# Adding pending squares on VectorE ahead of the norm sums, and the last store on ScalarE's queue

## The chip, the core and the metric

One NeuronCore of a Trainium2 chip runs the kernel: TensorE (PE, matmuls and their weight loads), VectorE (DVE), ScalarE (ACT), GpSimd (POOL) and the queues that issue DMAs, among them SyncE's (SP). The engines run side by side, each through its own instructions in order, and wait for each other by semaphores. The metric is the device time of one execution in microseconds; the median of several runs is given.

## What is computed

A two-layer decoder trunk on 512 tokens of width 1024, in float32. Layer 0 mixes by sliding-window attention and a convolution, layer 1 by a state-space scan; behind each mixer stands a gated ConvFFN, and at the end an RMS norm. What matters here are the norms, one behind each mixer and each ConvFFN:

```python
def rmsnorm(x, g):
    xf = x.astype(jnp.float32)
    y = xf * lax.rsqrt(jnp.mean(xf * xf, axis=-1, keepdims=True) + NORM_EPS)
    return (y * g.astype(jnp.float32)).astype(x.dtype)
...
        h = rmsnorm(x, norm_mix[i]) * (1.0 + sc_m) + sh_m
        ...
        x = x + g_m * y
        h = rmsnorm(x, norm_ffn[i]) * (1.0 + sc_f) + sh_f
        x = x + g_f * conv_ffn(h, ffn_w_gate[i], ffn_conv_w[i], ffn_conv_b[i],
                               ffn_w_val[i], ffn_w_down[i])
    return rmsnorm(x, final_norm)
```

## The kernel before

The residual stream `x` lies transposed in on-chip memory: 8 tiles of 128 features by 512 tokens. A weight tile comes by DMA as float32 (`raw`); ScalarE rounds it to a coarser type (`wh`, L317) and VectorE makes the rest (`wl`, L322). A product of one weight tile and one activation tile is three matmuls (L370 to L372: high times high, high times low, low times high).

Between two phases stands `boundary` (L476), called four times: behind the mixer of layer 0, its ConvFFN, the mixer of layer 1, and the last ConvFFN, where the final norm and the stores follow. It gets the weights of the phase's last output tiles (four behind a mixer, two behind a ConvFFN), and works them off twice, for the first 256 tokens (half 0) and the second 256 (half 1), so that the norm of half 0 can run beside the products of half 1.

- `products` (L486) makes one output tile of one half on TensorE. `finish` (L495) adds it to `x` on VectorE (L474, `residual`), and has ScalarE square the new `x` (L501) into a fresh tile. The squares are added up in `acc` (tile `ssq`), which already holds those of the phase's earlier output tiles. `finish` adds the square of the tile before (L499, VectorE), except behind the last tile: so two squares per half are still pending when the norm begins, those of the last two output tiles, in the list `sq[hf]`.
- `norm_steps` (L505) is a generator of the norm's small steps. Its first step calls `token_sums` (L391) on `acc` and the pending squares: for each source tile and each of the two groups of 128 tokens of the half, a matmul with a column of ones (L396), six matmuls into one PSUM tile of 128 by 2. Each such matmul shows as two passes in the trace. Then ScalarE takes the root (L508), VectorE refines its inverse by a Newton step (L510 to L516), and TensorE spreads the result over all partitions (L404).
- The first four steps for half 0 are issued out of `products` of half 1, once a quarter of its matmuls are issued (`SUMS_AT` 0.25), the spread at 0.65 (`REST_AT`). Just before, `W.ahead()` (L522) prepares the next weight tiles, which puts L317 on ScalarE's queue and L322 on VectorE's.
- The norm of half 1 is begun behind the last residual and two groups of the next phase's first matmuls (`first`, which makes three output tiles). Between its steps the modulated tiles `hn` of half 0 are made (`fill`, L460 on VectorE, L461 on ScalarE, L467 on VectorE).
- In the last boundary `fill` is that of `final` (L1818): per half, GpSimd multiplies two of the eight output tiles, VectorE the other six (L1828), in pairs. SP's queue stores the pairs of VectorE (L1832), in half 1 the last pair as two single tiles (L1830); ScalarE's queue stores GpSimd's pair (L1834).

PE, ACT, DVE and POOL run what the program issues in the order in which it is written (`manual_schedule`).

Of the kernel before, what the change touches and what calls it, by code (L numbers as in the profile page):

```python
# [21 lines left out]
ALU = mybir.AluOpType  # L22
# [202 lines left out]
def trunk(ctx: ExitStack, tc: tile.TileContext, xT_d, vecs_d, rows_d, dsk_d, pos_d, const_d, wss_d, wg0_d,  # L225
          w_d, wmod_d, wdt_d, out_d):
    nc = tc.nc
# [11 lines left out]
    def nm(s):  # L239
        uid[0] += 1  # L240
        return f"{s}{uid[0]}"

    def tmp(shape=(P, T), dt=F32):
        return tp.tile(list(shape), dt, tag="tmp", name=nm("tmp"))

    def bank(shape=(P, T)):
        return pp.tile(list(shape), F32, tag="ps", name=nm("ps"))

    def small(n, dt=F32):
        return sp.tile([P, n], dt, tag="sm", name=nm("sm"), bufs=24)  # L250
# [9 lines left out]
    tt = nc.vector.tensor_tensor  # L260
# [108 lines left out]
    def mm3(ps, w, ah, al, first, last):  # L369
        mm(ps, lhsT=w[0], rhs=ah, start=first, stop=False)  # L370
        mm(ps, lhsT=w[0], rhs=al, start=False, stop=False)  # L371
        mm(ps, lhsT=w[1], rhs=ah, start=False, stop=last)  # L372
# [9 lines left out]
    def step(gen, n=1):  # L382
        for _ in range(n):
            next(gen, None)

    def drain(gen):
        for _ in gen:
            pass


    def token_sums(srcs, n=NCH):  # L391

        ps = bank((P, n))
        for k, t_ in enumerate(srcs):
            for c in range(n):
                mm(ps[:, c:c + 1], lhsT=t_[:, c * P:(c + 1) * P], rhs=ones,  # L396
                   start=(k == 0 and c == 0), stop=(k == len(srcs) - 1 and c == n - 1))
        return ps

    def spread(col, n=NCH):  # L400

        ps = bank((P, n * P))
        for c in range(n):
            mm(ps[:, c * P:(c + 1) * P], lhsT=col[:, c:c + 1].broadcast_to([P, P]), rhs=ident,  # L404
               start=True, stop=True)
        return ps
# [31 lines left out]
    HALF = (slice(0, T // 2), slice(T // 2, T))  # L438
# [34 lines left out]
    def residual(ps, m, gate, hs=slice(0, T)):  # L473
        stt(x[:, m, hs], ps, gate(m), x[:, m, hs], ALU.mult, ALU.add)  # L474

    def boundary(ws, ms, acts, gate, acc, nxt, after=None):  # L476

        n = len(acts)
        ms = list(ms)
        sq = [[], []]
        ss, y = [None, None], [None, None]

        def products(hf, i, at=None):  # L486
            hs = HALF[hf]
            o = bank((P, T // 2))
            for kt in range(n):
                mm3(o, ws[i][kt], acts[kt][0][:, hs], acts[kt][1][:, hs], kt == 0, kt == n - 1)  # L490
                if at is not None:
                    at((i * n + kt + 1) / (len(ws) * n))
            return o

        def finish(hf, i, o):  # L495
            hs = HALF[hf]
            residual(o, ms[i], gate, hs)
            if len(sq[hf]) > 1 or (sq[hf] and i < len(ws) - 1):
                tt(acc[:, hs], acc[:, hs], sq[hf].pop(0), ALU.add)  # L499
            sq[hf].append(tmp((P, T // 2)))  # L500
            act(sq[hf][-1], x[:, ms[i], hs], AF.Square)  # L501
            if after is not None:
                after(ms[i], hs)

        def norm_steps(hf):  # L505
            s_ = token_sums([acc[:, HALF[hf]], *sq[hf]], 2)
            sd, v, y_, a, y2 = (small(2) for _ in range(5))
            act(sd, s_, AF.Sqrt, scale=1.0 / 1024.0, bias=eps[:, 0:1])  # L508
            yield
            ts(v, s_, 1.0 / 1024.0, 1e-6, ALU.mult, ALU.add)  # L510
            nc.vector.reciprocal(y_, sd)
            tt(a, y_, y_, ALU.mult)
            yield
            stt(a, a, -0.5, v, ALU.mult, ALU.mult)
            yield
            stt(y2, a, 1.5, y_, ALU.add, ALU.mult)  # L516
            yield
            y[hf] = spread(y2, 2)

        for i in range(len(ws)):  # L520
            finish(0, i, products(0, i))
        W.ahead()  # L522
        norm0 = norm_steps(0)
        hn, fill, nfirst = nxt()

        def at(f):
            if f >= SUMS_AT and ss[0] is None:
                ss[0] = True
                step(norm0, 4)
            if f >= REST_AT and y[0] is None:  # L530
                step(norm0)

        for i in range(len(ws)):
            o = products(1, i, at)
            if i < len(ws) - 1:
                finish(1, i, o)
        fill0 = fill(0, y[0])
        step(fill0, 3)
        finish(1, len(ws) - 1, o)
        wf = [W.take_only() for _ in range(nfirst)]  # L540
        outs = [bank() for _ in range(nfirst)]

        def first(hf, kt):
            hs = HALF[hf]
            for o_, w in zip(outs, wf):
                mm3(o_[:, hs], w[kt], hn[kt][0][:, hs], hn[kt][1][:, hs], kt == 0, kt == KT - 1)

        norm1 = norm_steps(1)
        if nfirst:
            first(0, 0)  # L550
            first(0, 1)
        step(norm1)
        step(fill0)
        if not nfirst:
            drain(fill0)
        for _ in range(3):
            step(norm1)
            step(fill0)
        drain(fill0)
        if nfirst:  # L560
            for kt in range(2, 5):
                first(0, kt)
        step(norm1)
        if nfirst:
            for kt in range(5, KT):
                first(0, kt)
        fill1 = fill(1, y[1])
        for kt in range(KT):
            step(fill1)
            if nfirst:  # L570
                first(1, kt)
        drain(fill1)
        return hn, outs
# [1244 lines left out]
    def final(fp):  # L1818
        def fill(hf, rb):
            hs = HALF[hf]  # L1820
            rs = fp.tile([P, T // 2], F32, tag="rs", name=nm("rs"), bufs=2)
            nc.scalar.copy(rs, rb)
            os_ = [fp.tile([P, 2, T // 2], F32, tag="o", name=nm("o"), bufs=8) for _ in range(4)]
            for k in range(2):
                nc.gpsimd.tensor_tensor(os_[0][:, k, :], x[:, k, hs], rs, ALU.mult)
            for n, kt in enumerate(range(2, 8)):
                o = os_[kt // 2]
                tt(o[:, kt % 2, :], x[:, kt, hs], rb, ALU.mult)  # L1828
                if hf and n > 3:
                    nc.sync.dma_start(out_d[:, kt:kt + 1, hs], o[:, kt % 2:kt % 2 + 1, :])  # L1830
                elif kt % 2:
                    nc.sync.dma_start(out_d[:, kt - 1:kt + 1, hs], o)  # L1832
                yield
            nc.scalar.dma_start(out_d[:, 0:2, hs], os_[0])  # L1834
        return None, fill, 0

    ctx.enter_context(tc.manual_schedule(engines={getattr(mybir.EngineType, e) for e in MANUAL}))
# [126 lines left out]
```

## Time and profile before

| | |
|---|---|
| median of 3 runs | 1341.47 us (1340.62 to 1342.1) |
| the profiled execution | 1342.0 us, span 1340.2 us |
| TensorE busy | 1313.2 us, 98% |
| VectorE busy | 875.1 us, 65% |
| ScalarE busy | 597.0 us, 45% |
| GpSimd busy | 74.7 us, 6% |
| mean granted clock of TensorE | 0.99 |

Times in the profile count from the first instruction of the profiled execution; its own time is 1.8 us longer than that span. A busy engine counts the time in which an instruction of it runs, and matmuls overlap: one of 256 columns shows 0.28 us and the next starts 0.12 us later. The four boundaries' norms lie at about 212, 578, 958 and 1324 us.

### The profile page before, as it was taken

How to read it: one execution, taken by the hardware profiler on the slowest of the kernel's cores; microseconds unless marked ns; L12 is line 12 of the kernel's file. 1: busy time of each engine (PE TensorE's matmuls, PEld its weight loads, DVE VectorE, ACT ScalarE, POOL GpSimd, SP SyncE). 2: the span in 40 equal slices, each digit the busy share in tenths (PEclk: the TensorE clock that was granted, in tenths of full speed). 3: DMA queues.
4: the chain of work that ended last, by engine and by line, in shares of the span. 5: the costliest groups of instructions: out<-in, count | busy, mean ns of one | idle time of the engine just before them, and what ended most of it. 6: DMA issues, size and time to landing. Idle time of an engine off the chain costs nothing.

```text
span 1340.2 us, 17613 instructions
## 1 busy us (share of the span) xinstructions
PE 1313.2 (98%) x6873; PEld 1078.0 (80%) x6873; DVE 875.1 (65%) x1342; ACT 597.0 (45%) x947; POOL 74.7 (6%) x129
## 2 busy tenths in 40 slices
PE   7999899999999999999999999999999999999997
PEld 6856589888888888897888887887988888888886
DVE  6976987775666676568686775878665434434443
ACT  4624734432233233347694764836353313322333
POOL 7010000000000000100110100000000000000002
PEclk8999899999999999999999999999999999999999
DMA  9773363564664665223542432342223233233311
GB/s 341 236 266 103 128 210 111 170 222 152 215 194 149 218 203 180 89 68 95 166 139 84 139 110 97 122 123 79 64 94 115 89 111 94 83 92 112 99 56 63
DMA packets 56436, 183.64 MB, mean 137 GB/s; under 512 B 7008, under 2 KB 10144, under 8 KB 56352
## 3 DMA queue, kind: packets, MB, share of 16 engines
q1 hardware_dynamic: 51536, 170.24, 39.5%
q0 software_dynamic: 4128, 11.61, 2.6%
q8 instruction: 54, 0.88, 0.3%
q10 hardware_dynamic: 688, 0.66, 0.1%
q14 instruction: 30, 0.25, 0.1%
HBM read 179.21 MB, written 3.28 MB: 136 GB/s over the span
## 4 chain that ended last, share of the span: by engine, by line
PE 93%; DVE 3%; ACT 2%; DMA 1%; issue 1%; DVEq 0%; ACTq 0%; POOLq 0%
PE ps L370 27%; PE ps L371 27%; PE ps L372 27%; PE ps L798 2%; PE ps L950 2%; PE ps L1643 1%; DMA M<-scr 1%; PE ps L1621 1%; PE ps L404 1%; PE ps L396 1%; PE ps L1609 1%; ACT M L1593 0%; PE ps L419 0%; PE ps L1108 0%; PE ps L1635 0%
## 5 line engine op out<-in xcount | busy, mean ns | idle before, releaser
L370 PE MATMUL ps<-hn,wh 128*128 128x512 f32 (+1 forms) x1214 | 460.2, 379 | 0.8 <-ACT hn L461 0.8
L371 PE MATMUL ps<-hn,wh 128*128 128x512 f32 (+1 forms) x1214 | 454.1, 374 | 0.4
L372 PE MATMUL ps<-hn,wl 128*128 128x512 f32 (+1 forms) x1214 | 453.9, 374 | 0.0
L322 DVE TENSOR_TENSOR wl<-raw,wh 128x1024 fp32r<-128x1024 f32 (+1 forms) x208 | 250.9, 1209 | 95.1 <-ACT wh L317 93.8
L317 ACT CAST wh<-raw 128x1024 fp32r<-128x1024 f32 (+1 forms) x208 | 213.1, 1027 | 221.5 <-PE ps L371 216.1
L370 PEld LDWEIGHTS ps<-hn,wh 128*128 128x128 f32 x1214 | 228.5, 188 | 44.6 <-issue 3.5
L371 PEld LDWEIGHTS ps<-hn,wh 128*128 128x128 f32 x1214 | 228.7, 188 | 42.3 <-issue 1.9
L372 PEld LDWEIGHTS ps<-hn,wl 128*128 128x128 f32 x1214 | 228.5, 188 | 40.7
L474 DVE SCALAR_TENSOR_TENSOR x<-ps,modv,x 128x512 f32<-128x512 f32 (+1 forms) x108 | 73.9, 690 | 115.2 <-PE ps L372 115.2
L370 PE MATMUL ps<-fh,wh 128*128 128x512 f32 (+1 forms) x380 | 142.2, 374 | 0.0
L371 PE MATMUL ps<-fl,wh 128*128 128x512 f32 (+1 forms) x380 | 141.9, 373 | 0.0
L372 PE MATMUL ps<-fh,wl 128*128 128x512 f32 (+1 forms) x380 | 141.9, 373 | 0.0
L595 DVE SCALAR_TENSOR_TENSOR mr<-mr,cb 128x1024 f32<-128x1024 f32 x92 | 111.1, 1219 | 1.6 <-DMA mr<-in_wmod_dram 1.6
L1346 ACT ACTIVATE tmp<-ps,vecs 128x512 f32<-128x512 f32 x44 | 34.2, 777 | 114.8 <-PE ps L372 114.8
L1347 DVE SCALAR_TENSOR_TENSOR tmp<-ps,vecs,tmp 128x511 f32<-128x511 f32 x44 | 32.9, 749 | 79.6 <-ACT tmp L1346 79.6
L370 PEld LDWEIGHTS ps<-fh,wh 128*128 128x128 f32 x380 | 71.5, 188 | 12.8
L372 PEld LDWEIGHTS ps<-fh,wl 128*128 128x128 f32 x380 | 71.5, 188 | 12.7
L371 PEld LDWEIGHTS ps<-fl,wh 128*128 128x128 f32 x380 | 71.5, 188 | 12.6
L295 ACT CAST fh<-tmp 128x512 fp32r<-128x512 f32 x44 | 27.3, 620 | 96.4 <-DVE tmp L1351 95.6
L449 POOL TENSOR_TENSOR ssq<-ssq,tmp 128x512 f32<-128x512 f32 x10 | 13.4, 1337 | 909.8 <-ACT tmp L448 909.8
L1349 ACT ACTIVATE tmp<-tmp 128x512 f32<-128x512 f32 x44 | 27.8, 632 | 75.6 <-DVE tmp L1348 75.5
L1593 ACT ACTIVATE M<-M,acs 128x128 f32<-128x128 f32 x128 | 39.6, 389 | 24.4 <-DMA M<-scr 24.3
(291 smaller groups left out, 1462.1 us busy)
## 6 DMA issues: line engine op xcount, KB each, us to landing
raw<-in_w_dram SPq DMA_DIRECT2D x176, 512.0 KB, 3.7
mr<-in_wmod_dram SPq DMA_DIRECT2D x80, 512.0 KB, 3.7
raw<-in_w_dram SPq DMA_DIRECT2D x32, 448.0 KB, 3.4
mr<-in_wss_dram SPq DMA_DIRECT2D x16, 512.0 KB, 7.2
M<-scr POOLq DMA_DIRECT2D x16, 512.0 KB, 4.6
s<-uc SPq DMA_DIRECT2D x16, 266.0 KB, 5.2
raw<-in_wg_dram SPq DMA_DIRECT2D x8, 384.0 KB, 7.5
E<-scr POOLq DMA_DIRECT2D x32, 96.0 KB, 3.7
```

The costliest lines, as they stand in the source:

```text
L295: nc.scalar.copy(h, src)
L317: nc.scalar.copy(h, self.raw[i].rearrange("p (k m) -> p k m", m=P))
L322: eng.tensor_tensor(l, self.raw[i].rearrange("p (k m) -> p k m", m=P), h.bitcast(F32), ALU.subtract)
L370: mm(ps, lhsT=w[0], rhs=ah, start=first, stop=False)
L371: mm(ps, lhsT=w[0], rhs=al, start=False, stop=False)
L372: mm(ps, lhsT=w[1], rhs=ah, start=False, stop=last)
L474: stt(x[:, m, hs], ps, gate(m), x[:, m, hs], ALU.mult, ALU.add)
L595: stt(raw, raw, 1.0, mod_pool[2], ALU.mult, ALU.mult, accum_out=out)
L1346: act(c, pg, AF.Identity, bias=vec("fcb", i), scale=vec("fcw", 3 * i + 2))
L1347: stt(c[:, 1:], pg[:, :T - 1], vec("fcw", 3 * i + 1), c[:, 1:], ALU.mult, ALU.add)
L1349: act(c, c, AF.Silu)
L1593: act(m_[:, i, c, :], m_[:, i, c, :], AF.Relu, bias=acs[:, c, h:h + 1], scale=-1.0)
```

## The change

At the start of `norm_steps`, VectorE adds pending squares into `acc` until none is left in half 0, and one in half 1. `token_sums` then has one source in half 0 (two matmuls in place of six) and two in half 1 (four in place of six). In half 1 of the last boundary, GpSimd's pair is stored ahead of the last single tile, and that tile's store goes to ScalarE's queue too.

```diff
         def norm_steps(hf):
+            while len(sq[hf]) > hf:
+                tt(acc[:, HALF[hf]], acc[:, HALF[hf]], sq[hf].pop(0), ALU.add)
             s_ = token_sums([acc[:, HALF[hf]], *sq[hf]], 2)
...
                 tt(o[:, kt % 2, :], x[:, kt, hs], rb, ALU.mult)
+                if hf and n == 5:
+                    nc.scalar.dma_start(out_d[:, 0:2, hs], os_[0])
                 if hf and n > 3:
-                    nc.sync.dma_start(out_d[:, kt:kt + 1, hs], o[:, kt % 2:kt % 2 + 1, :])
+                    (nc.scalar if n == 5 else nc.sync).dma_start(out_d[:, kt:kt + 1, hs], o[:, kt % 2:kt % 2 + 1, :])
                 elif kt % 2:
                     nc.sync.dma_start(out_d[:, kt - 1:kt + 1, hs], o)
                 yield
-            nc.scalar.dma_start(out_d[:, 0:2, hs], os_[0])
+            if not hf:
+                nc.scalar.dma_start(out_d[:, 0:2, hs], os_[0])
```

Lines behind L505 move down by two, so the new adds are L507, the root L510 and the Newton step L512 to L518.

VectorE in the first boundary, from the residual of half 0's last tile (L474) on. `wl_2066` is the rest of a weight tile, `ssq_129` is `acc`, `tmp_2039` and `tmp_2055` are the two pending squares. Before:

```order
L474 SCALAR_TENSOR_TENSOR x<-ps_2041,modv,x 128x256
L322 TENSOR_TENSOR wl_2066<-raw_2057,wh_2065 128x1024
L510 TENSOR_SCALAR sm_2106<-ps_2098 128x2
L511 RECIPROCAL sm_2107<-sm_2105 128x2
L512 TENSOR_TENSOR sm_2108<-sm_2107 128x2
```

and after the change:

```order
L474 SCALAR_TENSOR_TENSOR x<-ps_2041,modv,x 128x256
L322 TENSOR_TENSOR wl_2066<-raw_2057,wh_2065 128x1024
L507 TENSOR_TENSOR ssq_129<-ssq_129,tmp_2039 128x256
L507 TENSOR_TENSOR ssq_129<-ssq_129,tmp_2055 128x256
L512 TENSOR_SCALAR sm_2104<-ps_2100 128x2
L513 RECIPROCAL sm_2105<-sm_2103 128x2
```

The two adds stand behind the weight split L322 and ahead of the Newton step. TensorE at the same place, where `ps_2085` is half 1's first tile, `ps_2098` the sums and `ps_2119` half 1's second tile. Before:

```order
L371 MATMUL ps_2085<-s_1611,wh_1835 128x256
L372 MATMUL ps_2085<-s_1610,wl_1836 128x256
L396 MATMUL ps_2098<-ones,ssq_129 128x1 x2
L396 MATMUL ps_2098<-ones,tmp_2039 128x1 x2
L396 MATMUL ps_2098<-ones,tmp_2055 128x1 x2
L370 MATMUL ps_2119<-s_1560,wh_1835 128x256
```

and after (the sums are `ps_2100`, the second tile `ps_2117`):

```order
L371 MATMUL ps_2085<-s_1611,wh_1835 128x256
L372 MATMUL ps_2085<-s_1610,wl_1836 128x256
L396 MATMUL ps_2100<-ones,ssq_129 128x1 x2
L370 MATMUL ps_2117<-s_1560,wh_1835 128x256
L371 MATMUL ps_2117<-s_1561,wh_1835 128x256
```

Four matmuls of the sums are gone; the two that are left read `ssq_129`, which the second add writes. The end of ScalarE's queue, with the spread's copy (L1822 before) and the store of GpSimd's pair of half 1. Before:

```order
L1834 DMA out_dram<-o_10763 128x2x256
L1822 COPY rs_10804<-ps_10801 128x256
L1834 DMA out_dram<-o_10806 128x2x256
L1959 UNCONDITIONAL_BRANCH
```

and after:

```order
L1839 DMA out_dram<-o_10752 128x2x256
L1824 COPY rs_10792<-ps_10789 128x256
L1832 DMA out_dram<-o_10794 128x2x256
L1834 DMA out_dram<-o_10797 128x256
L1964 UNCONDITIONAL_BRANCH
```

The store of the last single tile (`o_10797`) stands behind that of GpSimd's pair (`o_10794`).

## Rows read from the trace of the kernel before

**Rows 1.** The page's busy table: busy us (share of span), instructions.
```profile
PE 1313.2 (98%) x6873; PEld 1078.0 (80%) x6873; DVE 875.1 (65%) x1342; ACT 597.0 (45%) x947; POOL 74.7 (6%) x129
```

**Rows 2.** Timeline, first boundary: start us, us, engine, line, operation [idle before it <-releaser].
```profile
211.36 0.42 ACT L501 ACTIVATE tmp<-x 128x256 f32<-128x256 f32 x1 [1.08 <-DVE x L474]
211.69 1.03 ACT L317 CAST wh<-raw 128x1024 fp32r<-128x1024 f32 x1
212.00 0.50 PE L396 MATMUL ps<-ones,ssq 128*128 128x1 f32 x4
212.36 1.03 PE L396 MATMUL ps<-ones,tmp 128*128 128x1 f32 x8
212.75 1.23 DVE L322 TENSOR_TENSOR wl<-raw,wh 128x1024 fp32r<-128x1024 f32 x1 [1.48 <-ACT wh L317]
...
213.26 0.37 PE L370 MATMUL ps<-s,wh 128*128 128x256 f32 x1
```

**Rows 3.** Timeline, second and third boundary, half 0: sums and weight split.
```profile
577.88 0.50 PE L396 MATMUL ps<-ones,ssq 128*128 128x1 f32 x4
...
578.61 1.23 DVE L322 TENSOR_TENSOR wl<-raw,wh 128x1024 fp32r<-128x1024 f32 x1 [1.48 <-ACT wh L317]
...
957.76 0.50 PE L396 MATMUL ps<-ones,ssq 128*128 128x1 f32 x4
...
958.49 1.23 DVE L322 TENSOR_TENSOR wl<-raw,wh 128x1024 fp32r<-128x1024 f32 x1 [1.48 <-ACT wh L317]
```

**Rows 4.** Instructions on tile `ssq`: count, ns min/median/max, first and last start us.
```profile
L499 DVE TENSOR_TENSOR ssq<-ssq,tmp x8: 415/418/426, 208.3 to 963.0; 128x256 f32<-128x256 f32 x8
```

**Rows 5.** Timeline, first boundary, half 0: root, last Newton step, spread.
```profile
214.03 0.26 ACT L508 ACTIVATE sm<-ps,eps 128x2 f32<-128x2 f32 x1
...
214.98 0.16 DVE L516 SCALAR_TENSOR_TENSOR sm<-sm,sm 128x2 f32<-128x2 f32 x1
...
215.83 0.61 PE L404 MATMUL ps<-con,sm 128*128 128x128 f32 x4
```

**Rows 6.** Timeline, first boundary, half 1: last residual, sums, Newton's first step.
```profile
220.60 0.48 DVE L474 SCALAR_TENSOR_TENSOR x<-ps,modv,x 128x256 f32<-128x256 f32 x1
...
221.29 0.50 PE L396 MATMUL ps<-ones,ssq 128*128 128x1 f32 x4
...
223.02 0.16 DVE L510 TENSOR_SCALAR sm<-ps 128x2 f32<-128x2 f32 x1 [1.16 <-ACT sm L508]
```

**Rows 7.** Timeline, last boundary: half 0's square and table load, half 1's residual and sums.
```profile
1323.00 0.42 ACT L501 ACTIVATE tmp<-x 128x256 f32<-128x256 f32 x1 [1.62 <-DVE x L474]
...
1323.98 1.28 ACT L508 ACT_TABLE_LOAD   x1
...
1329.23 0.48 DVE L474 SCALAR_TENSOR_TENSOR x<-ps,modv,x 128x256 f32<-128x256 f32 x1
...
1330.27 0.61 PE L396 MATMUL ps<-ones,tmp 128*128 128x1 f32 x4 [0.30 <-ACT tmp L501]
```

**Rows 8.** Timeline: SP's last stores; then windows: us, busy by engine, PEclk, DMA share, GB/s.
```profile
1335.15 1.52 SPq L1830 DMA_DIRECT2D out_dram<-o  x2
...
1335.00:1338.00 3.00, 0.00 (x0) 0.00 (x0) 0.32 (x1) 0.00 (x0) 0.00 (x0) 0.50 1.03 339
1338.00:1340.00 2.00, 0.00 (x0) 0.00 (x0) 0.00 (x0) 0.00 (x0) 0.00 (x0) 0.50 0.02 5
```

**Rows 9.** Windows: us, busy (x) of PE, PEld, DVE, ACT, POOL, PEclk, DMA share, GB/s.
```profile
152.00:156.00 4.00, 0.61 (x8) 0.23 (x6) 3.93 (x10) 2.92 (x5) 0.00 (x0) 1.00 0.83 286
156.00:168.00 12.00, 11.20 (x56) 7.53 (x58) 11.42 (x29) 10.02 (x27) 0.00 (x0) 0.57 0.40 121
218.00:220.00 2.00, 1.44 (x10) 1.03 (x10) 1.82 (x6) 1.37 (x3) 0.00 (x0) 1.00 0.28 63
906.00:908.00 2.00, 0.40 (x2) 0.00 (x0) 1.22 (x2) 2.00 (x6) 0.00 (x0) 1.00 0.00 0
```

## The prediction

> **What bounds the kernel now.** I read the page's busy table first: TensorE is busy for 98% of the span [rows 1], so whatever holds TensorE up for a microsecond makes the kernel longer by about that much, and what another engine does beside it costs nothing. Then the timeline at the four norms that sit inside a `boundary` call, since the change touches nothing else. At the first of them [rows 2] TensorE runs product matmuls, the sums (L396, twelve passes: three sources, two columns, two passes each), and product matmuls again without a pause; the reader is to see that ScalarE's last square ended at 211.36 + 0.42 = 211.78, before TensorE came to the sums at 212.00, and that VectorE begins a weight split (L322) only at 212.75. The next two boundaries, at 578 and 958 us, have the same rows [rows 3]. The fourth, ahead of the final norm, ends the kernel: there TensorE is no longer the bound, and the time runs through residual, square, sums, root, Newton step, spread, multiply and store [rows 7, 8].
>
> **First halves of the first three boundaries.** The change takes two of the three sources away from the sums: eight of twelve passes. Twelve passes put 213.26 - 212.00 = 1.26 us between the first of them and the next product [rows 2], 0.105 us each, so eight are worth 0.84 us. What it adds is two VectorE adds of the form that L499 has already, 0.418 us each [rows 4]. They are two more instructions of VectorE, and where they stand decides. In the built program they stand behind the L322 split on VectorE's queue, and the sums on TensorE now read the tile that the second add writes. Before, the sums needed squares that were there. After:
> - first boundary: L322 ends at 212.75 + 1.23 = 213.98, the two adds at 214.82; TensorE, ready at 212.00, waits 2.82 us, less 0.84 saved: 1.98;
> - second: 578.61 + 1.23 + 0.84 = 580.68 against 577.88: 2.80, less 0.84: 1.96 [rows 3];
> - third: 958.49 + 1.23 + 0.84 = 960.56 against 957.76: 1.96 [rows 3].
>
> Together **+5.9 us**. Queued behind the waiting sums on TensorE are the second half's products, in program order, so nothing fills the wait. The bounds: the adds may overlap what stands before them by up to 0.1 us each (the tail of L322), and a restart of an idle TensorE costs at most 0.11 us (four passes alone last 0.61 us, four in the stream 0.50 [rows 2, 7]): 5.3 to 6.3.
>
> Does the wait come back? The root, Newton step and spread follow the sums. Newton ended at 214.98 + 0.16 = 215.14 and the spread began at 215.83, when TensorE got there [rows 5]. After the change the sums end about 215.3, the root starts then instead of at 214.03 and Newton ends about 1.3 us later, at 216.4; TensorE reaches the spread about 2 us later, at 217.8. So the spread stays paced by TensorE, and all behind it moves with TensorE. The shift is kept.
>
> **Second halves of the first three boundaries.** One add stands directly behind the last residual (L474) on VectorE, ahead of two steps of the modulation. The residual ends at 220.60 + 0.48 = 221.08, the add at 221.50; TensorE comes to the sums at 221.29 [rows 6] and waits 0.21 us, but four passes fewer give back 0.42: -0.2 at each, **-0.6 us** in all. The add's 0.42 us on VectorE push the modulation steps back; VectorE had 1.16 us of idle time right after them, waiting for the root [rows 6], and that hides it. Bounds for each: -0.4 (no wait) to +0.4 (that cover is missing and the whole add delays the normalized tiles): -1.3 to +1.3 in all.
>
> **The fourth boundary.** In its first half no L322 stands ahead of the adds. The second add can start when the square ends, 1323.00 + 0.42, and ends near 1323.9. ScalarE is then still loading its table, until 1323.98 + 1.28 = 1325.26 [rows 7], and the root comes after that: nothing for the end, whether TensorE waits or not. In its second half the chain does pass the sums. Before, only the last four passes waited for the square, from 1330.27 to 1330.88 [rows 7]. After, the tile of the older squares comes from an add behind the residual: 1329.23 + 0.48 + 0.42 = 1330.13. Then come eight passes, and eight in a stream last 1.03 us [rows 2]: 1331.16, **+0.3 us**. Bounds 0 (the add overlaps the residual's tail) to +0.45.
>
> **The last store.** It goes to ScalarE's queue, behind the store of POOL's two tiles, instead of being the second of SP's two last stores, which together take 1.52 us from 1335.15 [rows 8]. But from 1335 to 1338 the DMA engines are full: 339 GB/s times 3.00 us is 1.02 MB, the whole half of the output (1.05 MB), and after 1338 nearly nothing moves [rows 8]. Issued earlier, the last piece waits for the same engines: **0**, with -0.4 (about one issue, half of the 1.52 us and less) and +0.2 (it is queued behind POOL's tiles) as bounds. The Trainium skill ("Trainium Kernel Development and Optimization", Key Constraints) says that the queues share the same DMA engines and that issuing from several only saves issue time; by that alone the term would be the saved issue, about -0.4, and the sum 0.4 us lower. The full engines in the rows speak for 0.
>
> **Sum.** 5.9 - 0.6 + 0.3 + 0 = +5.6 us. The profiled execution took 1342.0 us, so it would take 1347.6; the median of the runs before is 1341.47, 0.5 below, so I forecast **1347.1 us**. The bounds: 5.3 - 1.3 + 0 - 0.4 = +3.6, and 6.3 + 1.3 + 0.45 + 0.2 = +8.2: 1345.1 to 1349.7.
>
> **Rivals.**
> - *The clock falls in the new waits.* TensorE was nearly idle from 152 to 156 (0.61 of 4 us busy), and the granted clock then went from 2.4 to 1.2 GHz: mean 0.57 over the next 12 us, so (1 - 0.57) x 12 x 2 = 10.3 us at half. With 0.40 of 2 us busy at 906 to 908 it stayed at 1.00 [rows 9]. A wait of 2.7 us amid dense work lies between the two. One fall would cost up to half of 10.3, 5.2 us: 1352.3; three 1362.7. That the waits are single and the work on both sides dense speaks against. Chance 0.12.
> - *Part of the shift is swallowed.* Behind the boundary TensorE waits again for normalized tiles, 0.56 us at 218 to 220 [rows 9]. If those tiles did not move with TensorE, three such gaps would take 1.7 us: 1345.4; with the other waits of that kind twice as much, 1343.7. Against it: the spread is paced by TensorE [rows 5]. 0.08.
> - *Not slower: the adds are done early.* VectorE is idle until 212.75, and the last square ends at 211.78 [rows 2]. If the adds ran in that gap they would end at 212.62, TensorE would wait 0.62 us and save 0.84: -0.2 at each place, in all -0.6 - 0.6 + 0.3 = -0.9, 1340.6; without any wait 3 x -0.84 - 0.3 = -2.8, 1338.7. It decides where the adds end before 212.84. The built order, with the split ahead of the adds, speaks against it. 0.08.
>
> **How the numbers follow.** The forecast has 0.72, the clock 0.12, the swallowed shift 0.08, early adds 0.08. Single runs before lie between 1340.62 and 1342.1, up to 0.63 above the median. The range takes in the forecast's bounds, most of the swallowed shift, and that spread at the upper end: **1344.5 to 1350.3**; it leaves out the clock and the early adds, 0.20. About 0.2% (2.7 us) is what can be told from no change, so slower means above 1344.2: 0.72 + 0.12 + 0.06 = 0.90; the same 0.02 + 0.04 = 0.06; faster 0.04.
>
> **What would show it.** In the profile after, the timeline at about 212, 580 and 962 us should show L322, two adds of 0.42 us, then four sum passes, and an idle time of 2.6 to 2.8 us on TensorE ended by VectorE's add; product matmuls again some 3 us after the last one. In the second halves a wait of about 0.2 us ended by the same add. In the last boundary eight passes after an add, and the final stores ending 3 us after the DMA engines fill, whichever queue issued the last. I am wrong if the adds end before TensorE arrives, if later waits shrink by as much as the new ones cost, or if the granted clock has a new stretch at half behind one of the waits.

## The result, and the profile after

The changed kernel takes 1351.64 us (median of 4 runs, 1350.97 to 1352.59) against 1341.78 us for the kernel before on the same chip: 1.0075 of it, 95% interval [1.0057, 1.0092], 9.9 us more. I had forecast 5.6 us more, and 1350.3 as the upper end of the range. The profiled execution took 1351.29 us, with a span of 1349.5. Of all executions reported below one, the profiled one of the last kernel (1871.56 us at a mean granted clock of 0.65), was in a slower state of the chip, and its kernel's ratio leaves it out.

The timeline of the changed kernel at the first boundary (start us, us, engine, line, operation, idle time before it and what ended that) answers to [rows 2] and [rows 5]:

```profile
210.02 1.23 DVE L322 TENSOR_TENSOR wl<-raw,wh 128x1024 fp32r<-128x1024 f32 x1 [1.48 <-ACT wh L317]
211.16 0.88 DVE L507 TENSOR_TENSOR ssq<-ssq,tmp 128x256 f32<-128x256 f32 x2
212.09 0.61 PE L396 MATMUL ps<-ones,ssq 128*128 128x1 f32 x4 [2.66 <-DVE ssq L507]
212.56 0.46 PE L370 MATMUL ps<-s,wh 128*128 128x256 f32 x1
...
215.17 0.41 PE L370 MATMUL ps<-s,wh 128*128 128x256 f32 x1
215.38 0.41 PE L371 MATMUL ps<-s,wh 128*128 128x256 f32 x1
...
216.18 0.28 PE L372 MATMUL ps<-s,wl 128*128 128x256 f32 x1
216.30 0.28 PE L370 MATMUL ps<-s,wh 128*128 128x256 f32 x1
...
216.65 0.61 PE L404 MATMUL ps<-con,sm 128*128 128x128 f32 x4
```

The reader is to see two things. First the forecast wait: split, two adds, and TensorE idle for 2.66 us until the second add is done. Then something that the sum did not have: the product matmuls behind the wait start 0.21 us apart (215.17 to 215.38) and not 0.12 us (216.18 to 216.30). The windows of the changed kernel (us, busy of PE, PEld, DVE, ACT and POOL, granted clock, DMA share, GB/s) say why:

```profile
209.00:211.00 2.00, 0.43 (x4) 0.23 (x2) 0.98 (x1) 1.98 (x3) 0.00 (x0) 1.00 0.00 0
211.00:213.00 2.00, 0.91 (x6) 0.91 (x7) 1.00 (x3) 0.55 (x2) 0.00 (x0) 0.92 0.42 66
213.00:215.00 2.00, 2.00 (x12) 2.00 (x11) 1.11 (x6) 0.42 (x1) 0.00 (x0) 0.50 0.48 197
215.00:217.00 2.00, 2.00 (x15) 2.00 (x15) 0.81 (x2) 0.42 (x1) 0.00 (x0) 0.73 0.00 0
...
580.00:582.00 2.00, 0.58 (x3) 0.61 (x4) 1.24 (x3) 0.53 (x1) 0.00 (x0) 0.83 0.36 53
582.00:584.00 2.00, 2.00 (x10) 2.00 (x11) 0.72 (x5) 0.26 (x1) 0.00 (x0) 0.50 0.52 209
584.00:586.00 2.00, 2.00 (x11) 2.00 (x11) 0.48 (x1) 0.42 (x1) 0.00 (x0) 0.50 0.05 12
586.00:588.00 2.00, 2.00 (x12) 2.00 (x11) 0.65 (x2) 0.14 (x1) 0.00 (x0) 0.50 0.00 0
588.00:590.00 2.00, 2.00 (x18) 2.00 (x18) 1.81 (x6) 1.28 (x3) 0.00 (x0) 0.96 0.00 0
...
966.00:968.00 2.00, 1.68 (x10) 1.68 (x11) 0.90 (x7) 0.26 (x1) 0.00 (x0) 0.75 0.57 193
968.00:970.00 2.00, 2.00 (x12) 2.00 (x11) 0.93 (x4) 0.42 (x1) 0.00 (x0) 0.50 0.17 70
970.00:972.00 2.00, 2.00 (x17) 2.00 (x17) 0.47 (x3) 0.42 (x1) 0.00 (x0) 0.89 0.00 0
```

At all three boundaries the granted clock goes from 2.4 to 1.2 GHz at the end of the wait or just behind it, for (0.08 + 0.50 + 0.27) x 2 x 2 = 3.4 us at the first, (0.17 + 3 x 0.50 + 0.04) x 2 x 2 = 6.8 us at the second and (0.25 + 0.50 + 0.11) x 2 x 2 = 3.4 us at the third. The kernel before had 1.00 there.

From the time at which TensorE was ready for the sums to the spread, the first boundary took 215.83 - 212.00 = 3.83 us before [rows 2, 5]. After, the last product matmul ended at 212.09 - 2.66 = 209.43. In a stream a product matmul shows 0.28 us and the next starts 0.12 us after its start, so 0.16 us ahead of its end: TensorE was ready at 209.27, and the sums came 2.82 us later. The spread began at 216.65: 7.38 us, **3.6 more**. The first product behind the sums came 212.56 - 209.27 = 3.29 us after that point, before 1.26 [rows 2]: 2.0 us is the wait less the passes saved, as forecast (1.98), and the other 1.5 us lie in the products at half the clock. At the second and third boundary, in the changed kernel

```profile
581.42 0.99 PE L396 MATMUL ps<-ones,ssq 128*128 128x1 f32 x4 [2.73 <-DVE ssq L507]
...
586.26 1.05 PE L404 MATMUL ps<-con,sm 128*128 128x128 f32 x4
...
966.32 0.61 PE L396 MATMUL ps<-ones,ssq 128*128 128x1 f32 x4 [2.64 <-DVE ssq L507]
...
970.89 0.61 PE L404 MATMUL ps<-con,sm 128*128 128x128 f32 x4
```

and in the kernel before, where the sums stand in [rows 3],

```profile
581.37 0.60 PE L404 MATMUL ps<-con,sm 128*128 128x128 f32 x4
...
961.61 0.60 PE L404 MATMUL ps<-con,sm 128*128 128x128 f32 x4
```

so, with TensorE ready at 581.42 - 2.73 - 0.16 = 578.53 and 966.32 - 2.64 - 0.16 = 963.52, 586.26 - 578.53 = 7.73 against 3.49, **4.2 more**, and 970.89 - 963.52 = 7.37 against 3.85, **3.5 more**. In the second boundary the half clock lasts beyond the spread and costs some 0.4 us more behind it.

These are 11.3 us; the span grew by 9.3. The profiled execution of the changed kernel came to the first boundary 2.7 us earlier (209.27 against 212.00), before any changed instruction. The stretch at half clock near 155 us, which both kernels have [rows 9], was 6.8 us long there and 10.3 before, but that is part of it at most: the kernel with only the store changed, below, has 3.4 us there and comes to its sums at 210.00. The rest is not explained. So single profiles are compared from point to point here, and kernels by medians.

### The profile page after: what moved, and what is told of

Same layout as the page of the kernel before. It is cut to its first block, busy times and chain, and to the rows that moved or that the text cites. A ratio compares the mean times of both kernels' runs of the same rounds, so it can differ in the third digit from the quotient of the medians.

```text
span 1349.5 us, 17531 instructions
## 1 busy us (share of the span) xinstructions
PE 1312.7 (97%) x6825; PEld 1077.0 (80%) x6825; DVE 879.7 (65%) x1354; ACT 596.6 (44%) x947; POOL 73.6 (5%) x129
## 4 chain that ended last, share of the span: by engine, by line
PE 90%; DVE 4%; ACT 3%; DMA 2%; issue 1%; DVEq 0%; ACTq 0%; POOLq 0%
PE ps L370 27%; PE ps L371 26%; PE ps L372 26%; PE ps L800 2%; PE ps L952 2%; DMA M<-scr 2%; PE ps L1645 1%; PE ps L1623 1%; DVE mr L597 1%; PE ps L404 1%; ACT M L1595 1%; PE ps L1611 1%; PE ps L1050 1%; PE ps L396 0%; DVE wl L322 0%
## 5 line engine op out<-in xcount | busy, mean ns | idle before, releaser
L322 DVE TENSOR_TENSOR wl<-raw,wh 128x1024 fp32r<-128x1024 f32 (+1 forms) x208 | 250.8, 1209 | 93.4 <-ACT wh L317 92.5
L474 DVE SCALAR_TENSOR_TENSOR x<-ps,modv,x 128x512 f32<-128x512 f32 (+1 forms) x108 | 74.0, 689 | 120.9 <-PE ps L372 120.9
```

What stands on the lines that cost most here:

```text
L322: eng.tensor_tensor(l, self.raw[i].rearrange("p (k m) -> p k m", m=P), h.bitcast(F32), ALU.subtract)
```

## The experiments

The theory behind the forecast: TensorE waits in the first halves, because the adds stand behind the weight split. What the trace added: the clock falls behind each wait. The rivals: other parts of the change carry the loss, or what I read as the clock's share is something else.

### Only the first halves' adds

```diff
         def norm_steps(hf):
+            while hf == 0 and sq[hf]:
+                tt(acc[:, HALF[hf]], acc[:, HALF[hf]], sq[hf].pop(0), ALU.add)
```

> Only the two adds per first half (the sums of the second halves keep their pending squares, the last store stays on SyncE's queue). Theory (the whole loss comes from TensorE's wait for these adds, 2.7 us each at three boundaries, and from a stretch at half clock behind each wait): 3 x 2.0 us for the waits plus 3 x 1.3 to 1.5 us for the clock, 10 us over the kernel before, 1351 to 1353 us, with three new stretches at 0.5 in the record of the granted clock at the boundaries. Rival (adds of the second halves and the last store carry the part of the loss that I had not forecast): about 6 us, 1347 to 1348.

Measured: 1353.39 us against 1339.62 on its chip, 1.0101 [1.0084, 1.0118]. The whole loss is in this part alone: 13.8 us, more than the changed kernel's own. The profile has idle times of 2.66, 2.73 and 2.64 us ended by L507, and a stretch at half clock of 3.4 us behind each of the three. It also has a fourth behind the idle time that the kernel before shows at 906 [rows 9], which was 1.82 us long here. From the start of the last product matmul ahead of the first half's sums to the second half's spread, the three boundaries took 17.55, 16.14 and 17.55 us in this trace, and 13.98, 12.63 and 14.01 in that of the kernel before: 10.6 of the 13.8 us. The time between the second and the third, where the fourth fall lies, was 1.4 us longer; the rest is not assigned. The rival falls.

### Only the second halves' adds

```diff
         def norm_steps(hf):
+            while hf == 1 and len(sq[hf]) > 1:
+                tt(acc[:, HALF[hf]], acc[:, HALF[hf]], sq[hf].pop(0), ALU.add)
```

> Only the one add per second half. Theory: a wait of some 0.2 us at TensorE less 0.42 us of passes at three boundaries, -0.2 each, and +0.3 us in the last boundary, where the sums lie on the chain to the end: -0.3 us, 1340.8 to 1342.2, no new stretch at half clock. Rival (the second halves' adds delay the modulated tiles): +1 to +4 us.

Measured: 1340.42 us against 1339.62, 1.0004 [0.9995, 1.0013]: no difference that can be told. The size of the parts is better read from the traces. In this kernel's own trace the three boundaries, measured as above, take 13.80, 12.45 and 13.82 us, each 0.2 less than before, and the last one 8.81 against 8.55, 0.3 more. In the changed kernel, at the first boundary and at the last:

```profile
221.42 0.47 DVE L474 SCALAR_TENSOR_TENSOR x<-ps,modv,x 128x256 f32<-128x256 f32 x1
221.82 0.41 DVE L507 TENSOR_TENSOR ssq<-ssq,tmp 128x256 f32<-128x256 f32 x1
...
222.28 0.61 PE L396 MATMUL ps<-ones,ssq 128*128 128x1 f32 x4
...
223.67 0.16 DVE L512 TENSOR_SCALAR sm<-ps 128x2 f32<-128x2 f32 x1 [0.65 <-ACT sm L510]
...
1338.23 0.48 DVE L474 SCALAR_TENSOR_TENSOR x<-ps,modv,x 128x256 f32<-128x256 f32 x1
1338.62 0.41 DVE L507 TENSOR_TENSOR ssq<-ssq,tmp 128x256 f32<-128x256 f32 x1
...
1339.09 0.60 PE L396 MATMUL ps<-ones,ssq 128*128 128x1 f32 x4 [1.26 <-DVE ssq L507]
...
1339.56 0.58 PE L396 MATMUL ps<-ones,tmp 128*128 128x1 f32 x4
```

From the residual to Newton's first step: 223.67 - 221.42 = 2.25 us, before 223.02 - 220.60 = 2.42 [rows 6], so -0.17 (forecast -0.2). VectorE's idle time there shrank from 1.16 to 0.65 us: the idle time that I had named as cover took the add. In the last boundary from the residual to the end of the sums: 1340.14 - 1338.23 = 1.91 us, before 1330.88 - 1329.23 = 1.65 [rows 7], so +0.26 (forecast +0.3).

### Only the last store

```diff
+                if hf and n == 5:
+                    nc.scalar.dma_start(out_d[:, 0:2, hs], os_[0])
                 if hf and n > 3:
-                    nc.sync.dma_start(out_d[:, kt:kt + 1, hs], o[:, kt % 2:kt % 2 + 1, :])
+                    (nc.scalar if n == 5 else nc.sync).dma_start(out_d[:, kt:kt + 1, hs], o[:, kt % 2:kt % 2 + 1, :])
...
```

> Only the last store on ScalarE's queue. Theory: the DMA engines are full from 1335 to 1338, so 0 within 0.4 us. Rival one (the last store's issue sets the end): -0.4 us or more, and the span after TensorE's last matmul gets shorter by that. Rival two (it is held up behind GpSimd's pair): +0.2 us or more.

Measured: 1339.72 us against 1339.62, 0.9997 [0.9987, 1.0007]. Time alone cannot tell 0 from -0.4; the trace of this kernel can (copy of the spread, last issue, and the windows of the end):

```profile
1330.67 0.37 ACT L1822 COPY rs<-ps 128x256 f32<-128x256 f32 x1 [1.66 <-PE ps L404]
...
1333.18 0.37 ACTq L1832 DMA_DIRECT2D out_dram<-o  x1
...
1333.00:1336.00 3.00, 0.00 (x0) 0.00 (x0) 0.15 (x1) 0.00 (x0) 0.00 (x0) 0.50 0.99 323
```

The copy to the end of the span takes 1338.1 - 1330.67 = 7.4 us, before 1340.2 - 1332.83 = 7.4. The last issue ended 2.9 us behind the start of the copy (1333.18 + 0.37 = 1333.55), before 3.8 (1336.67 [rows 8]): it came 0.9 us earlier, the DMA engines were as full as before, and the end did not move.

### The wait kept, TensorE kept busy

TensorE gets matmuls to do in the wait whose product nobody reads; all the rest is the changed kernel.

```diff
             while len(sq[hf]) > hf:
                 tt(acc[:, HALF[hf]], acc[:, HALF[hf]], sq[hf].pop(0), ALU.add)
+            if hf == 0 and nfirst:
+                idle = bank((P, T // 2))
+                for k in range(21):
+                    mm(idle, lhsT=ws[-1][k % n][0], rhs=acts[k % n][0][:, HALF[1]], start=k == 0, stop=k == 20)
```

> The changed kernel with 21 extra matmuls of 256 columns (21 x 0.12 = 2.5 us) on TensorE ahead of the first halves' sums at the first three boundaries; their product is not used. The adds, their place on VectorE and the time at which the sums may start stay; only TensorE is not idle in the wait. Theory (clock): no stretch at 0.5 behind the waits, so 2.0 us each are left and 1.3 to 1.5 us each go: 3.5 to 4.5 us faster than the changed kernel, 1347 to 1348 us. Rival (the loss beyond 6 us is not the clock's): 1351 to 1352, as the changed kernel.

Measured: 1345.54 us against 1339.62, 1.0041 [1.0025, 1.0057], 5.9 us more. Sums and spread at the three boundaries, and a window at the first, in this kernel:

```profile
212.12 0.61 PE L396 MATMUL ps<-ones,ssq 128*128 128x1 f32 x4 [0.18 <-DVE ssq L507]
...
215.16 0.61 PE L404 MATMUL ps<-con,sm 128*128 128x128 f32 x4
...
579.93 0.58 PE L396 MATMUL ps<-ones,ssq 128*128 128x1 f32 x4 [0.22 <-DVE ssq L507]
...
582.60 0.60 PE L404 MATMUL ps<-con,sm 128*128 128x128 f32 x4
...
961.65 0.60 PE L396 MATMUL ps<-ones,ssq 128*128 128x1 f32 x4
...
964.71 0.60 PE L404 MATMUL ps<-con,sm 128*128 128x128 f32 x4
...
213.00:215.00 2.00, 2.00 (x19) 2.00 (x18) 1.78 (x8) 0.58 (x3) 0.00 (x0) 1.00 0.42 170
```

The sums still start when the add is done, yet the clock stays at 1.00 at all three boundaries. The kernel does more work than the changed one and is faster. By the medians some 4 us of the loss are the clock's (9.9 less 5.9, each known to within 2.4 us), and what is left, 5.9 us, is near the forecast's own sum of 5.6. The traces say it more sharply: from the sums to the spread, 3.04, 2.67 and 3.06 us here, in the changed kernel 4.56, 4.84 and 4.57. That is 1.5, 2.2 and 1.5 us, 5.2 together, for the clock up to the spreads.

The changed kernel itself, run again beside the next two:

> The changed kernel once more, so that the other kernels of this set have it on the same chip. Theory (three waits of 2.7 us and a fall of the clock behind each): 10 to 13 us over the kernel before, at least three stretches at half clock behind the boundaries. Rival (the kernel with only the first halves' adds was slower than this one because second halves' adds and the store gain something): 10 us or less.

Measured: 1351.06 us against 1340.86, 1.0073 [1.0057, 1.0089]: 10.2 us, as the first time. The fall at 914 us that the first experiment had is in this profile too; the one of the first measurement did not have it.

With 10 extra matmuls, and with 15 (`range(10)`, `range(15)` in the diff above, `stop` to match):

> As the kernel with 21 extra matmuls in each wait, with 10: TensorE is idle for about 2.7 - 10 x 0.12 = 1.5 us at a stretch, and the time at which the sums may start is the same. If the clock falls only behind the long idle time: as with 21, 5 to 6.5 us over the kernel before, no stretch at half clock at the boundaries. If any wait of this kind makes it fall: 9 to 13 us, as the changed kernel.

> As the kernels with 21 and with 10 extra matmuls in each wait, with 15: TensorE idle for about 2.7 - 15 x 0.12 = 0.9 us. If the clock's fall goes with the idle time and 0.9 us is little enough: 5 to 6.5 us over the kernel before, as with 21, no stretch at half clock at the boundaries. If it still falls: 9 to 13 us, as with 10.

Measured: with 10, 1352.65 against 1340.86 us, 1.0084 [1.0070, 1.0098]; with 15, 1345.59 against 1340.0, 1.0042 [1.0026, 1.0058]. First boundary with 10 (timeline, windows):

```profile
213.71 0.61 PE L396 MATMUL ps<-ones,ssq 128*128 128x1 f32 x4 [1.49 <-DVE ssq L507]
...
215.00:217.00 2.00, 2.00 (x13) 2.00 (x12) 1.53 (x6) 0.58 (x2) 0.00 (x0) 0.56 0.36 147
217.00:219.00 2.00, 2.00 (x13) 2.00 (x12) 0.07 (x1) 0.25 (x1) 0.00 (x0) 0.58 0.00 0
```

and with 15:

```profile
212.34 0.61 PE L396 MATMUL ps<-ones,ssq 128*128 128x1 f32 x4 [0.89 <-DVE ssq L507]
...
213.00:215.00 2.00, 2.00 (x18) 2.00 (x18) 1.59 (x7) 0.66 (x2) 0.00 (x0) 1.00 0.56 223
215.00:217.00 2.00, 2.00 (x19) 2.00 (x18) 1.04 (x3) 0.45 (x2) 0.00 (x0) 1.00 0.00 0
```

| extra matmuls | idle before the sums, three boundaries | falls of the clock there | over the kernel before, medians | the three boundaries over the kernel before, traces |
|---|---|---|---|---|
| 0 | 2.66, 2.73, 2.64 us | 3 of 3 | 9.9 and 10.2 us | 11.1 and 11.2 us |
| 10 | 1.49, 1.54, 1.45 us | 3 of 3 | 11.8 us | 10.1 us |
| 15 | 0.89, 0.94, 0.84 us | 0 of 3 | 5.6 us | 5.6 us |
| 21 | 0.18, 0.22, 0.12 us | 0 of 3 | 5.9 us | 5.6 us |

The last column is the time from the start of the last product matmul ahead of the first half's sums (the extra matmuls do not count) to the second half's spread. By it half of the changed kernel's loss is the waits' and half the clock's.

That 1.5 us of idle time would be harmless was one of the two outcomes that I had named, and it was not: the loss goes in one step, between 0.9 and 1.5 us of idle time at these places. That is no general bound: in the kernel with only the store changed TensorE was idle for 1.98 us at 904 without a fall, and with 15 extra matmuls 1.99 us at 909 was followed by one. The kernel with 10 has a fall there too, behind 2.23 us. And in a kernel below, the one with later sums, 2.26 us at the first boundary's spread was not followed by one.

### The adds ahead of the weight split

The order on VectorE, not the adds, should be the cause. Here `norm_steps` finds the first half's squares already added:

```diff
         for i in range(len(ws)):
             finish(0, i, products(0, i))
+        for t_ in sq[0]:
+            tt(acc[:, HALF[0]], acc[:, HALF[0]], t_, ALU.add)
+        sq[0].clear()
         W.ahead()
```

> The changed kernel with the first halves' two adds issued ahead of the next weight tile's split on VectorE; second halves and store as in the changed kernel. Theory (the split ahead of the adds makes the wait): the adds run while VectorE was idle and end near 212.65, TensorE waits about 0.65 us in place of 2.66 and saves 0.84: -0.2 us each, with second halves and last boundary -1 to +1 us against the kernel before, no new stretch at half clock. Rival (the adds themselves cost it): 3 us or more over the kernel before.

Measured: 1339.57 us against 1340.86, 0.9991 [0.9981, 1.0000]. Timeline at the first boundary:

```profile
208.95 0.42 DVE L525 TENSOR_TENSOR ssq<-ssq,tmp 128x256 f32<-128x256 f32 x1
...
209.58 0.43 DVE L525 TENSOR_TENSOR ssq<-ssq,tmp 128x256 f32<-128x256 f32 x1 [0.21 <-ACT tmp L501]
...
210.06 0.61 PE L396 MATMUL ps<-ones,ssq 128*128 128x1 f32 x4
...
210.51 1.23 DVE L322 TENSOR_TENSOR wl<-raw,wh 128x1024 fp32r<-128x1024 f32 x1 [0.51 <-ACT wh L317]
```

The same two adds run in the time in which VectorE waited for the rounded weights, the split starts no later, and the long wait is gone with the falls of the clock. Some 0.3 us of it are left: the sums begin 0.41 us after the start of the last product matmul, 0.12 us in a stream. By this trace the three boundaries, measured as in the table, take 13.38, 12.18 and 13.30 us, 0.6, 0.5 and 0.7 less than before, and the last one 8.96, 0.4 more: some 1.3 us less in all, as the medians say. It is the loss of 10 us turned into a gain of about 1, which the medians alone can just tell, by the place of two instructions.

Two versions try to make more of it, both on the kernel before. The first also issues the sums later (`SUMS_AT` 0.375 in place of 0.25), so that not even the short wait is left:

> The kernel before with the first halves' two adds ahead of the weight split, and the sums issued after 0.375 of the second half's matmuls in place of 0.25, so 0.72 us later; second halves and store as before. Theory: no wait at the sums, eight passes of 0.105 us saved at three boundaries and hidden in the fourth: -2.5 us against the kernel before. Rival (the later sums make the spread wait for the Newton step, or moving passes does not shorten TensorE's stream): 0 or slower.

Measured: 1341.61 us against 1340.86, 1.0013 [1.0003, 1.0023]. The rival was right, and the trace names the place:

```profile
209.86 0.50 PE L396 MATMUL ps<-ones,ssq 128*128 128x1 f32 x4
...
211.61 0.42 ACT L501 ACTIVATE tmp<-x 128x256 f32<-128x256 f32 x1 [1.75 <-DVE x L474]
212.04 1.28 ACT L508 ACT_TABLE_LOAD   x1
213.34 0.26 ACT L508 ACTIVATE sm<-ps,eps 128x2 f32<-128x2 f32 x1
...
214.51 0.71 PE L404 MATMUL ps<-con,sm 128*128 128x128 f32 x4 [2.26 <-DVE sm L516]
```

Sums issued within the second product put the root, and the table load ahead of it, behind a square on ScalarE's queue; in the kernel before it stood ahead of that square. The root came late, and TensorE waited 2.26 us at the first boundary's spread, 0.42 and 0.80 us at the next two: the wait had only moved.

The second takes what each part gave by itself: early adds in the first halves, the second halves' add at the first three boundaries alone, sums and store as before.

> The kernel before with the first halves' adds ahead of the weight split, the second halves' add at the first three boundaries only, and the store as before. Theory: -0.5 us at each first half, -0.2 at each second half, nothing in the last boundary: -2 us, 0.9985 of the kernel before. Rival (the adds give nothing once they are out of the way): within 0.5 us of the kernel before.

Measured: 1338.38 us against 1340.0, 0.9988 [0.9977, 1.0000], 1.6 us less (interval 0 to 3.1): the forecast 2 us less lies within it, and so does the rival's half a microsecond. It is ahead of the kernel before by no more than the measurement can just tell, as the changed kernel with early adds is; which of the two is better is not shown. No trace of it is read.

## Why the prediction was wrong

- **The wait.** The step was right at each place: forecast 2.82, 2.80 and 2.80 us from TensorE's arrival to the sums, measured 2.82, 2.89 and 2.80 (idle times of 2.66, 2.73 and 2.64 us and the 0.16 us ahead of the last product's end); net of the saved passes 1.98 forecast and 2.0 measured at the first. That it is the order on VectorE is shown by the kernel with early adds.
- **Does the wait come back.** Right: nothing behind swallowed it. The kernels with 15 and 21 extra matmuls, in which only the wait is left, lie 5.6 and 5.9 us above the kernel before, and the sum said 5.6. That the medians come so close is partly luck, as each is known to within some 2 us; by the traces the three boundaries cost 5.6 us in both, where the sum had 5.9 - 0.6 = 5.3.
- **Second halves, last boundary, store.** -0.17, +0.26 and 0 by the traces against -0.2, +0.3 and 0.
- **The clock.** This is the step that failed. I had it as a rival with a chance of 0.12 and left it out of the range; it happened at all three boundaries, in both measurements of the changed kernel. It was also mis-sized: 5.2 us for one fall, taken from a stretch of 10.3 us, where the three falls lasted 3.4, 6.8 and 3.4 us and cost 4 us together by the medians, 5.6 by the traces (11.2 less 5.6). What misled me were the idle times of the kernel before. I read 906 to 908, 0.40 of 2 us busy with the clock at 1.00, as a sign that a wait between it and the one at 152 to 156 would probably do no harm, and "single waits in dense work" as an argument. The kernel with 10 extra matmuls shows that at these boundaries 1.5 us, less than that very gap, were followed by a fall each time. So the gap at 906 said nothing on these waits, and what decides whether a fall follows stays open.
- **The last sentence of the prediction** named a new stretch at half clock behind one of the waits as what would make it wrong. That is what the profile shows.

## What to carry to other kernels

An instruction that another engine waits for belongs ahead of any long instruction on its own queue that nobody waits for yet; when work is moved from one engine to another, read what stands in front of it there before pricing the work itself. Where TensorE is the bound and runs without a pause, price a new wait twice: its own length, and up to half of the stretch at half clock that may follow (here 1.5 us of 3.4), and put the second into the range unless a wait as long at the same place is known to be harmless. Before moving a small step on one queue, look at every other queue on which it has a part: the later sums lost on ScalarE's queue what they had won on TensorE's.

## What the runs showed of the hardware

The clock's fall came with an idle time of 1.5 us at these places in three of three, and did not with 0.9 us in three of three. Idle times of 1.8 to 2.3 us at 904 to 915 were followed by a fall in some profiles and not in others, in kernels that do the same there, and 2.26 us at a spread was not; what decides between them is open. And TensorE doing 15 or 21 useless matmuls in each of three waits made the kernel some 4 us faster than leaving it idle by the medians, 5.6 us by the traces of the three boundaries.
